# mLSTM: half of the output gate moves to heads 4 to 7, their keys and queries into heads 0 to 3, and a head's sums follow the next scores

## The chip, the cores and the metric

One core of a Trainium2 chip runs the whole program; the other cores are idle. The metric is the device time of one execution in microseconds (us). The engines of the core work side by side, each on its own queue of instructions: TensorE (PE, the matrix products; PEld are its weight loads), VectorE (DVE), ScalarE (ACT), GpSimd (POOL) and SyncE (SP), which issues the loads of the weights.

## The reference, cut to what matters

A trunk of two layers over 512 tokens and 1024 features. Each layer is half a SwiGLU feed-forward, a mixer, and another half feed-forward. The mixer of the first layer is an mLSTM with 8 heads, that of the second a sparse attention (NSA) whose keys and values are computed once, between the two. The mLSTM, in the parts that the change touches:

```python
proj = h @ w_in
q, k, v, ig, fg, og = split(proj)              # 8 heads: q, k of 64, v of 128 columns; og 1024
log_f = log_sigmoid(fg + b_f); b = cumsum(log_f)
D = b[t] - b[s] + log_i[s]                     # for s <= t
W = exp(D - m_t) * (q @ k.T)
num = W @ v + ...                              # and the state carried over chunks
den = sum(W, -1) + ...
h_out = rmsnorm(num / max(abs(den), exp(-m_t)))
return (h_out * sigmoid(og)) @ w_out
```

Between the layers, blocks of the keys and of the values are compressed: `silu(flat @ w1) @ w2`.

## The kernel before

All tokens of the sequence stay in SBUF, transposed: `h[b]` holds 128 features by 512 tokens. Products are made exact to nearly float32 by splitting each operand into a high part and a remainder (`split`: the high part on ScalarE, the difference on VectorE) and adding three matmuls, hi x hi, hi x lo and lo x hi (`mm3`). Weights go the same way: `load_weight` fetches a strip of 512 KB with a DMA on SP into one of two buffers `wraw`, ScalarE writes `whi`, VectorE `wlo`, three buffers each; a strip is asked for two ahead of its use.

The program is written as generators whose steps are one `mm3` or so. `weave(main, fill, ratio)` runs `main` and puts `ratio` steps of `fill` behind each of its steps, so that TensorE has other products while a chain of small work runs on the other engines. The instruction scheduler of the framework may then still change the order within an engine.

In the mLSTM the stages follow each other like this: the input gate products and the first keys and queries; `gates()`, a long chain of row operations on VectorE that ends in `um` (rows of the decay exponents), which TensorE transposes into `pnm`; `project_qk(0)` (keys and queries of heads 0 to 3), `project_v(0)`; then `heads(0)` (heads 0 to 3), filled by `project_og()` (the output gate, eight strips of eight steps); the sigmoids of all eight strips; `project_qk(1)`; `project_v(1)` with `finish(0)`; `heads(1)` (heads 4 to 7), filled by `project_out(0)` (the output projection of heads 0 to 3, 32 steps); `finish(1)`; `project_out(1)`.

A head does this: `S`, the scores, on TensorE; `decay(h + 1)` brings the next head's exponents (`pnm`, then `dg` on VectorE and `E` on ScalarE); VectorE multiplies `E` by `S`; `split` gives `Wh` and `Wl`; GpSimd adds the four strips of `E` into the first (L486); TensorE multiplies by v into `pn`; ScalarE copies that to `num` and squares it to `sqn`. `total` then splits the sums of `E` and `sqn` into `th` and `tl` (ScalarE, VectorE) and adds them with one matmul each into the bank `dm`, so four `dm` matmuls a head. `finish` reads `dm`, makes the scale of each token, and for each head scales `num` (VectorE), multiplies by `sig` (GpSimd, L533) and splits it into `yhi` and `ylo`, which lie in the same eight buffers as the mixer's input x (`xhi`, `xlo`).

`kv()` runs beside the feed-forward `ffn2`: it compresses the blocks in steps between which the feed-forward fills in. `nsa()` begins with `project_q(0)` and the scale `rc` of the tokens from the sum of squares.

## Time and profile before

| | us |
|---|---|
| median of 3 runs | 2067.87 (2067.59 to 2068.0) |
| the profiled execution | 2072.25 |
| its span, first to last instruction | 2070.5 |
| TensorE busy | 2032.7 (98%) |
| VectorE busy | 1155.9 (56%) |
| ScalarE busy | 782.3 (38%) |
| GpSimd busy | 161.1 (8%) |

The profile is of one execution; its times of single instructions and stretches belong to the 2072.25 us, while the runs are timed without it. The mean granted clock of TensorE is 0.996. Matmuls are pipelined: a row's length is longer than the distance to the next one's start, and a busy TensorE can still run below its peak.

### The profile page before, as it was taken

Reading aid. Unit: us, or ns where it says so; the run is one execution under the profiler, and the core shown is the slowest. Engines: PE = TensorE matmul, PEld = TensorE weight load, DVE = VectorE, ACT = ScalarE, POOL = GpSimd, SP = SyncE. Lnnn points to the kernel's source line nnn. Section 1 sums busy time; section 2 is a strip of 40 time slices with the busy share of each in tenths; the row PEclk is TensorE's granted clock in tenths of the full one; section 3 lists DMA queues with packets and bytes.
Section 4 is the critical chain, followed back from the end, with each engine's and each line's share of the span. In section 5 each row is a group of like instructions: output and inputs, shape, how many; then the busy total and the mean of one; then the engine's idle time right before and its main releaser. Section 6 shows DMA issues by size and latency. Waiting matters only on the chain.

```text
span 2070.5 us, 24480 instructions
## 1 busy us (share of the span) xinstructions
PE 2032.7 (98%) x9460; PEld 1666.6 (80%) x9460; DVE 1155.9 (56%) x2044; ACT 782.3 (38%) x1296; POOL 161.1 (8%) x171
## 2 busy tenths in 40 slices
PE   8999999999989999999999999999999999999999
PEld 6888888778768888888887888887778788888887
DVE  6434445765874444445566434446899985444443
ACT  5323223445653222234343322223667663223231
POOL 1000000011220000000101000001333310000000
PEclk9999999999999999999999999999999999999999
DMA  4232323323112323333333332323111112323322
GB/s 160 92 102 91 102 94 91 94 84 100 62 62 92 99 95 97 97 99 97 100 101 125 104 100 86 108 92 100 45 55 42 42 52 93 100 93 97 98 98 94
DMA packets 56468, 188.12 MB, mean 91 GB/s; under 512 B 6816, under 2 KB 7456, under 8 KB 56352
## 3 DMA queue, kind: packets, MB, share of 16 engines
q1 hardware_dynamic: 55392, 184.47, 27.9%
q8 instruction: 74, 1.21, 0.2%
q0 software_dynamic: 384, 1.05, 0.2%
q10 hardware_dynamic: 576, 1.05, 0.1%
q14 instruction: 42, 0.34, 0.1%
HBM read 177.10 MB, written 2.10 MB: 87 GB/s over the span
## 4 chain that ended last, share of the span: by engine, by line
PE 89%; DVE 6%; ACT 2%; issue 1%; POOL 1%; DMA 0%; SPq 0%; ACTq 0%; DVEq 0%; POOLq 0%
PE pmm L142 79%; PE S L142 3%; PE po L142 2%; PE pt L879 1%; PE vps L142 1%; PE paux L142 1%; DVE wlo L124 1%; POOL E L486 1%; DVE qh L762 0%; DVE pr L845 0%; DVE rq L219 0%; DVE ptl L152 0%; PE dm L142 0%; ACT xhi L186 0%; DVE Wl L152 0%
## 5 line engine op out<-in xcount | busy, mean ns | idle before, releaser
L123 ACT ACTIVATE whi<-wraw 128x1024 fp32r<-128x1024 f32 (+4 forms) x399 | 359.9, 916 | 995.4 <-PE pmm L142 821.2
L142 PE MATMUL pmm<-xhi,whi 128*128 128x512 f32 x1672 | 657.6, 393 | 7.7 <-ACT whi L123 7.7
L142 PE MATMUL pmm<-xlo,whi 128*128 128x512 f32 x1672 | 653.9, 391 | 0.0
L142 PE MATMUL pmm<-xhi,wlo 128*128 128x512 f32 x1672 | 653.8, 391 | 0.0
L124 DVE TENSOR_TENSOR wlo<-wraw,whi 128x1024 fp32r<-128x1024 f32 (+4 forms) x399 | 421.0, 1065 | 79.2 <-ACT whi L123 70.7
L142 PEld LDWEIGHTS pmm<-xhi,whi 128*128 128x128 f32 x1672 | 314.5, 188 | 70.6 <-ACT whi L123 8.9
L142 PEld LDWEIGHTS pmm<-xhi,wlo 128*128 128x128 f32 x1672 | 314.3, 188 | 66.8 <-DVE wlo L124 1.1
L142 PEld LDWEIGHTS pmm<-xlo,whi 128*128 128x128 f32 x1672 | 314.6, 188 | 61.8
L142 PE MATMUL pmm<-ghi,wlo 128*128 128x512 f32 x704 | 273.9, 389 | 0.0
L142 PE MATMUL pmm<-ghi,whi 128*128 128x512 f32 x704 | 273.9, 389 | 0.0
L142 PE MATMUL pmm<-glo,whi 128*128 128x512 f32 x704 | 273.9, 389 | 0.0
L270 DVE TENSOR_TENSOR fu<-pmm,r 128x512 f32<-128x512 f32 x88 | 60.8, 691 | 260.5 <-PE pmm L142 260.3
L308 DVE SCALAR_TENSOR_TENSOR h<-pmm,h 128x512 f32<-128x512 f32 x96 | 66.2, 691 | 250.1 <-PE pmm L142 250.1
L268 DVE TENSOR_TENSOR ft<-pmm,r 128x512 f32<-128x512 f32 x88 | 60.8, 690 | 174.2 <-PE pmm L142 174.2
L142 PEld LDWEIGHTS pmm<-glo,whi 128*128 128x128 f32 x704 | 132.2, 188 | 27.5
L142 PEld LDWEIGHTS pmm<-ghi,whi 128*128 128x128 f32 x704 | 132.2, 188 | 27.4
L142 PEld LDWEIGHTS pmm<-ghi,wlo 128*128 128x128 f32 x704 | 132.2, 188 | 27.4
L197 POOL TENSOR_TENSOR ssq<-ssq,sq 128x512 f32<-128x512 f32 x18 | 27.6, 1531 | 1019.5 <-ACT sq L196 1019.5
L151 ACT ACTIVATE ghi<-ft 128x512 fp32r<-128x512 f32 x88 | 55.7, 633 | 72.9 <-DVE ft L271 72.8
L846 ACT ACTIVATE pr<-pr,nx 128x512 f32<-128x512 f32 (+3 forms) x128 | 70.6, 554 | 8.6 <-DVE pr L845 7.9
L152 DVE TENSOR_TENSOR glo<-ft,ghi 128x512 fp32r<-128x512 f32 x88 | 60.4, 686 | 14.7 <-ACT ghi L151 14.7
L845 DVE TENSOR_SCALAR_CACHE_REDUCE pr<-S,cn 128x512 f32<-128x512 f32 (+3 forms) x128 | 66.1, 537 | 2.6 <-PE S L142 2.5
(299 smaller groups left out, 2068.3 us busy)
## 6 DMA issues: line engine op xcount, KB each, us to landing
wraw<-in_ffn_in SPq DMA_DIRECT2D x176, 512.0 KB, 3.5
wraw<-in_ffn_out SPq DMA_DIRECT2D x64, 448.0 KB, 3.3
wraw<-in_ffn_out SPq DMA_DIRECT2D x32, 512.0 KB, 3.6
wraw<-in_m_qk SPq DMA_DIRECT2D x8, 512.0 KB, 3.4
wraw<-in_m_v SPq DMA_DIRECT2D x8, 512.0 KB, 3.6
wraw<-in_m_og SPq DMA_DIRECT2D x8, 512.0 KB, 3.5
wraw<-in_m_out SPq DMA_DIRECT2D x8, 512.0 KB, 3.5
wraw<-in_kv_t SPq DMA_DIRECT2D x8, 512.0 KB, 3.5
```

The lines of the kernel that those rows point to most:

```text
L123: nc.scalar.activation(hi[:p, c], raw[:p, c], AF.Copy)
L124: nc.vector.tensor_tensor(lo[:p, c], raw[:p, c], hi[:p, c].bitcast(F32), op=ALU.subtract)
L142: self.nc.tensor.matmul(out, lhsT, rhs, start=start, stop=stop)
L151: self.nc.scalar.activation(hi, src, AF.Copy)
L152: self.nc.vector.tensor_tensor(lo, src, hi.bitcast(F32), op=ALU.subtract)
L197: (nc.gpsimd if b < 4 else nc.vector).tensor_tensor(t, t, sq, op=ALU.add)
L268: nc.vector.tensor_tensor(t, pa, r, op=ALU.mult)
L270: nc.vector.tensor_tensor(u, pb, r, op=ALU.mult)
L308: nc.vector.scalar_tensor_tensor(h, po[j], 0.5, h, op0=ALU.mult, op1=ALU.add)
L486: nc.gpsimd.tensor_tensor(E[:, sb * P:T], E[:, sb * P:T], E[:, SEG[sb]:SEG[sb] + T - sb * P], op=ALU.add)
L845: TS(s, S[:, i, :n], cc, None, op0=ALU.mult, op1=ALU.min, accum_out=nx[:, i:i + 1])
L846: nc.scalar.activation(s, s, AF.Exp, bias=nx[:, i:i + 1], scale=-1.0, accum_out=z[:, i:i + 1])
```

## The change

The two stops of `gates()` are new: the generator halts before `um`'s transposes, and 20 steps of `project_v(0)` are placed ahead of these. `project_og` takes a half, four strips. The filling work of `heads(0)` is og's strips 0 to 3 and then `project_qk(1)` (64 steps, as before with eight strips of og); that of `heads(1)` is og's strips 4 to 7 and then `project_out(0)`, at 1.05 steps for each step of the heads, in place of 0.4. The sigmoids come in two groups of four, the second behind `heads(1)`, with a table load of its own. `total` no longer issues its matmuls; `add_sums` does, behind the scores of the next head. In `kv()` and `nsa()` the stops between steps change.

```diff
             def gates():
                 ...
                 TS(t2, t2, -1.0, None, op0=ALU.mult)
+                yield
                 nM = pair("nM", t2)
                 up = ps_nm()[:, :160].rearrange("p (t c) -> p t c", t=NTB)
                 ...
-                return nM, uc, e2
+                yield nM, uc, e2
-            def project_og():
-                for m in range(KB):
+            def project_og(half):
+                for m in range(4 * half, 4 * half + 4):
             def heads(half):
                 first = 4 * half
-                E = decay(first)
+                E, sums = decay(first), []
                 def total(row, src, last, *tags):
                     hi, lo = (self.sp.tile([P, T], F32R, name=n, tag=t, bufs=k) for n, (t, k) in zip(("th", "tl"), tags))
                     self.split(src, hi, lo)
-                    for t in (hi, lo):
-                        self.mm(d, hot[:, 39 - row:167 - row], t, row == first and t is hi, last and t is lo)
+                    sums.append((row, hi, lo, last))
+                def add_sums():
+                    while sums:
+                        row, hi, lo, last = sums.pop(0)
+                        for t in (hi, lo):
+                            self.mm(d, hot[:, 39 - row:167 - row], t, row == first and t is hi, last and t is lo)
                 for h in range(first, first + 4):
                     ...
                         yield
+                    add_sums()
                     nE = decay(h + 1) if h < first + 3 else None
                     ...
                     yield
+                add_sums()
+                yield
-            og, out0 = project_og(), project_out(0)
             qk0 = project_qk(0)
             for _ in range(KB):
                 next(qk0)
             r = self.rstd_rows(rc, ps_nm())
-            nM, uc, e2 = gates()
+            g = gates()
+            next(g)
             run(qk0)
-            run(project_v(0))
-            weave(heads(0), og, 1.5)
-            run(og)
-            for m in range(KB):
-                tc.keep_in_program_order(nc.scalar.activation(sig[m], sig[m], AF.Sigmoid))
-            run(project_qk(1))
+            v0 = project_v(0)
+            for _ in range(20):
+                next(v0)
+            nM, uc, e2 = next(g)
+            run(v0)
+            def sigmoids(half):
+                for m in range(4 * half, 4 * half + 4):
+                    tc.keep_in_program_order(nc.scalar.activation(sig[m], sig[m], AF.Sigmoid))
+            rest = chain(project_og(0), project_qk(1))
+            weave(heads(0), rest, 1.45)
+            run(rest)
+            sigmoids(0)
             weave(project_v(1), finish(0), 0.25)
-            weave(heads(1), out0, 0.4)
-            weave(finish(1), out0, 1)
-            run(out0)
+            rest = chain(project_og(1), project_out(0))
+            weave(heads(1), rest, 1.05)
+            sigmoids(1)
+            weave(finish(1), rest, 4)
+            run(rest)
             run(project_out(1))
         # kv: three stops where one was, ahead of the first weight's products (w1)
                     self.split(F.rearrange("p i h c -> p i (h c)"), Fh, Fl)
-                    yield
+                    for _ in range(3):
+                        yield
         # kv: two stops behind the silu, three behind hh
                 nc.scalar.activation(hid[:n], hp[:n], AF.Silu)
-                yield
+                for _ in range(2):
+                    yield
                 ...
                 self.split(ht.rearrange("p k h g c -> p k h (g c)"), hh, hl)
-                yield
+                for _ in range(3):
+                    yield
         # nsa
             rc, var = self.rstd_columns(ssq, ps_t())
+            q1 = project_q(1)
+            for _ in range(4):
+                next(q1)
             run(q0)
             ...
-            for _ in project_q(1):
-                front.steps(0.6)
+            for _ in q1:
+                front.steps(1.2)
```

The order of instructions differs from before within the mLSTM, in the compression beside `ffn2`, and in NSA from its start on. Three places in it:

TensorE at the gates, before: `vps` are the products of v, `um` the rows to be transposed into `pnm`. 52 matmuls of v stand ahead of the transposes.

```order
L142 MATMUL vps<-whi,xlo 128x512
L142 MATMUL vps<-whi,xhi 128x512
L379 MATMUL pnm<-cst,um 128x40 x4
L142 MATMUL vps<-wlo,xhi 128x512
L142 MATMUL vps<-whi,xlo 128x512
```

After, the same place, the transposes between other products of v:

```order
L143 MATMUL vps<-wlo,xhi 128x512
L143 MATMUL vps<-whi,xlo 128x512
L381 MATMUL pnm<-cst,um 128x40 x4
L143 MATMUL vps<-whi,xhi 128x512
L143 MATMUL vps<-wlo,xhi 128x512
```

The transposes stand behind 60 matmuls of v in place of 52.

TensorE among heads 4 to 7, before, from the end of one head's `pn` on (`S` scores, `dm` the sums, `pnm<-nM` the next head's exponents, `pmm` filling work):

```order
L142 MATMUL pn<-Wh,vl 128x256
L142 MATMUL dm<-th,hot 128x512
L142 MATMUL pnm<-nM,sel 128x512
L142 MATMUL pmm<-ylo,whi 128x512
L142 MATMUL dm<-tl,hot 128x512
L142 MATMUL pmm<-yhi,wlo 128x512
L142 MATMUL pmm<-yhi,whi 128x512
L142 MATMUL pmm<-ylo,whi 128x512
L142 MATMUL pmm<-yhi,wlo 128x512
L142 MATMUL S<-qh,kk 128x512
L142 MATMUL S<-ql,kk 128x512
L142 MATMUL dm<-th,hot 128x512
```

The first sum of the head stands right behind its `pn`. After, from the last two matmuls of a head's scores on:

```order
L143 MATMUL S<-qh,kk 128x256
L143 MATMUL S<-ql,kk 128x256
L143 MATMUL pmm<-xhi,whi 128x512
L143 MATMUL pmm<-xlo,whi 128x512
L143 MATMUL pmm<-xhi,wlo 128x512
L143 MATMUL dm<-th,hot 128x512
L143 MATMUL dm<-tl,hot 128x512
L143 MATMUL dm<-th,hot 128x512
L143 MATMUL dm<-tl,hot 128x512
L143 MATMUL pnm<-nM,sel 128x512
L143 MATMUL pmm<-xhi,whi 128x512
```

The four `dm` matmuls of a head were spread from behind its own `pn` into the next scores; now they stand together behind the next head's scores, ahead of `pnm`.

VectorE among heads 4 to 7, before, in one head's stretch (`tl` and `Wl` remainders of a split, `dg` the exponents on the diagonal, `E` times the scores, `h` the residual):

```order
L483 TENSOR_TENSOR E<-E,S 128x512
L450 SCALAR_TENSOR_TENSOR dg<-pnm,uc,cst 128x128
L483 TENSOR_TENSOR E<-E,S 128x512
L152 TENSOR_TENSOR tl<-sqn,th 128x512
L450 SCALAR_TENSOR_TENSOR dg<-pnm,uc,cst 128x128
L483 TENSOR_TENSOR E<-E,S 128x256
L152 TENSOR_TENSOR Wl<-E,Wh 128x512 x2
L450 SCALAR_TENSOR_TENSOR dg<-pnm,uc,cst 128x128
L152 TENSOR_TENSOR Wl<-E,Wh 128x256
```

Nothing of the filling work stands there. After, at the head in which the output projection of heads 0 to 3 begins:

```order
L491 TENSOR_TENSOR E<-E,S 128x512
L441 TENSOR_TENSOR sig<-pmm,r 128x512
L125 TENSOR_TENSOR wlo<-wraw,whi 128x512 x2
L153 TENSOR_TENSOR ylo<-num,yhi 128x512
L491 TENSOR_TENSOR E<-E,S 128x512
L153 TENSOR_TENSOR ylo<-num,yhi 128x512
L491 TENSOR_TENSOR E<-E,S 128x256
L153 TENSOR_TENSOR ylo<-num,yhi 128x512
L452 SCALAR_TENSOR_TENSOR dg<-pnm,uc,cst 128x128
L153 TENSOR_TENSOR tl<-sqn,th 128x512
L153 TENSOR_TENSOR ylo<-num,yhi 128x512
L452 SCALAR_TENSOR_TENSOR dg<-pnm,uc,cst 128x128
```

The four `ylo` of heads 0 to 3 and the `sig` and `wlo` of og's strips stand among the head's own instructions, where before there were fewer of others. On TensorE, 21 dense matmuls stand between the transposes of `hid` and the first `paux<-hh` of the first compression, where nine stood.

## Rows read from the trace of the kernel before

**Rows 1.** The page: the span, and part 1 of it for TensorE, VectorE, ScalarE and GpSimd (busy us, share of the span, instructions).

```profile
span 2070.5 us, 24480 instructions
...
PE 2032.7 (98%) x9460; PEld 1666.6 (80%) x9460; DVE 1155.9 (56%) x2044; ACT 782.3 (38%) x1296; POOL 161.1 (8%) x171
```

**Rows 2.** The chain of waits over the whole execution, one row of it: start, length in us, engine, tile and line, number of instructions.

```profile
21.89 350.28 PE pmm L142 x1552
```

**Rows 3.** Busy time by stretch of the span. Columns: stretch, its length, then busy us (instructions) of TensorE, its weight loads, VectorE, ScalarE and GpSimd, then the granted TensorE clock, the share of DMA and GB/s.

```profile
372.00:430.00 58.00, 55.52 (x241) 43.87 (x240) 44.50 (x75) 23.10 (x42) 0.09 (x1) 0.94 0.33 101
430.00:495.00 65.00, 63.67 (x295) 51.12 (x294) 43.43 (x72) 34.87 (x76) 10.49 (x12) 1.00 0.20 66
495.00:540.00 45.00, 44.68 (x201) 36.12 (x200) 29.69 (x54) 22.37 (x41) 5.95 (x5) 1.00 0.36 107
540.00:585.00 45.00, 40.73 (x188) 32.30 (x187) 37.35 (x75) 30.33 (x68) 11.26 (x12) 0.96 0.13 46
585.00:620.00 35.00, 30.87 (x125) 23.09 (x124) 26.20 (x40) 17.47 (x28) 10.70 (x7) 0.95 0.22 75
...
1055.00:1105.00 50.00, 46.48 (x226) 38.36 (x225) 29.43 (x41) 21.58 (x36) 3.01 (x2) 0.97 0.37 111
...
1442.00:1460.00 18.00, 16.33 (x95) 12.32 (x93) 10.20 (x33) 7.70 (x10) 3.18 (x3) 1.00 0.30 90
```

**Rows 4.** The timeline at the gates, first TensorE, then VectorE: start, length, engine, line, operation, tiles, shapes; in square brackets the idle time before it and what ended that.

```profile
415.64 0.61 PE L379 MATMUL pnm<-cst,um 40*128 40x40 f32 x4 [2.48 <-DVE um L374]
...
414.81 0.68 DVE L374 TENSOR_TENSOR um<-t,t 8x512 f32<-8x512 f32 x1
```

**Rows 5.** Busy time by stretch around the same place, then among heads 4 to 7, columns as in rows 3.

```profile
413.00:425.00 12.00, 9.52 (x31) 7.54 (x31) 6.48 (x10) 3.16 (x7) 0.00 (x0) 0.72 0.40 131
...
563.00:566.00 3.00, 3.00 (x10) 2.38 (x10) 3.00 (x8) 2.70 (x9) 0.85 (x1) 0.57 0.01 5
```

**Rows 6.** VectorE in 540 to 585 us by line: line, operation, tiles, shapes, count | busy us, mean ns | idle time before.

```profile
L152 DVE TENSOR_TENSOR Wl<-E,Wh 128x512 fp32r<-128x512 f32 (+1 forms) x12 | 9.0, 771 | 0.2 <-ACT Wh L151 0.2
L483 DVE TENSOR_TENSOR E<-E,S 128x512 f32<-128x512 f32 (+1 forms) x12 | 6.9, 590 | 0.0
...
L450 DVE SCALAR_TENSOR_TENSOR dg<-pnm,uc,cst 128x128 f32<-128x128 f32 x16 | 5.5, 344 | 1.7 <-ACT E L452 1.7
...
L152 DVE TENSOR_TENSOR tl<-E,th 128x512 fp32r<-128x512 f32 x4 | 2.8, 692 | 2.0 <-ACT th L151 1.7
```

**Rows 7.** VectorE in 430 to 495 us by line, columns as in rows 6.

```profile
L124 DVE TENSOR_TENSOR wlo<-wraw,whi 128x512 fp32r<-128x512 f32 x16 | 11.6, 749 | 0.0
```

**Rows 8.** The waits: of TensorE in 540 to 585, of its weight loads in 540 to 585, and of its weight loads in 430 to 495 us. Columns: what waited for what, us in total, times, longest.

```profile
PE dm L142 <- ACT th L151: 4.0, 4, 1.6
...
PEld dm L142 <- ACT th L151: 5.5, 5, 1.8
...
PEld pn L142 <- DVE Wl L152: 2.2, 4, 1.0
PEld dm L142 <- DVE tl L152: 1.7, 4, 0.5
```

**Rows 9.** The timeline, columns as in rows 4: ScalarE and TensorE among heads 4 to 7, then a pair on VectorE among heads 0 to 3 with GpSimd beside it, then such a pair among heads 4 to 7.

```profile
560.47 0.63 ACT L151 ACTIVATE th<-E 128x512 fp32r<-128x512 f32 x1 [1.78 <-POOL E L486]
...
561.21 0.57 ACT L497 COPY num<-pn 128x512 f32<-128x512 f32 x1
...
562.47 0.63 ACT L151 ACTIVATE th<-sqn 128x512 fp32r<-128x512 f32 x1
...
561.15 0.50 PE L142 MATMUL dm<-th,hot 128*128 128x512 f32 x1 [1.61 <-ACT th L151]
...
438.06 2.41 DVE L152 TENSOR_TENSOR Wl<-E,Wh 128x512 fp32r<-128x512 f32 x2
...
438.02 2.76 POOL L486 TENSOR_TENSOR E<-E 128x384 f32<-128x384 f32 x3 [65.93 <-DVE Wl L152]
...
564.39 1.28 DVE L152 TENSOR_TENSOR Wl<-E,Wh 128x512 fp32r<-128x512 f32 x2
```

**Rows 10.** VectorE in 495 to 516 us by line, columns as in rows 6.

```profile
L152 DVE TENSOR_TENSOR ql<-qks,qh 64x512 fp32r<-64x512 f32 x4 | 2.7, 682 | 0.1
...
L396 DVE SCALAR_TENSOR_TENSOR qks<-pmm,r 128x512 f32<-128x512 f32 x2 | 1.4, 688 | 2.1 <-PE pmm L142 2.1
```

**Rows 11.** The timeline of GpSimd at the end of the mLSTM, columns as in rows 4.

```profile
593.76 1.66 POOL L533 TENSOR_TENSOR num<-num,sig 128x512 f32<-128x512 f32 x1 [1.29 <-DVE num L532]
```

**Rows 12.** The timeline of ScalarE at the sigmoids, columns as in rows 4.

```profile
492.60 1.28 ACT L562 ACT_TABLE_LOAD   x1
493.89 4.28 ACT L562 ACTIVATE sig<-sig 128x512 f32<-128x512 f32 x8
```

**Rows 13.** The compression: the timeline of TensorE (columns as in rows 4), a stretch (columns as in rows 3), and from the page the loads of the weights in question (count, KB each, us to landing).

```profile
1095.87 0.38 PE L676 MATMUL paux<-cst,hid 124*128 124x124 f32 x2
...
1101.00 0.33 PE L142 MATMUL paux<-hh,wlo 128*128 128x128 f32 x1 [2.21 <-DVE wlo L124]
...
1101.00:1107.00 6.00, 6.00 (x22) 5.02 (x23) 4.11 (x9) 2.23 (x4) 0.40 (x1) 0.72 0.55 175
...
wraw<-in_c_w SPq DMA_DIRECT2D x8, 512.0 KB, 3.6
```

**Rows 14.** The waits of TensorE in 1442 to 1452 us, columns as in rows 8.

```profile
PE pt L142 <- DVE rq L220: 1.7, 1, 1.7
```

More of the change, by code (lines that the diff above doesn't have):

```diff
@@ L2 @@
 from contextlib import ExitStack
+from itertools import chain
 import numpy as np
```

## The prediction

> **What bounds the kernel now.** I first read the page: TensorE is busy for 2032.7 of 2070.5 us, VectorE for little over half of that [rows 1]. So TensorE's work is nearly the whole time, and since the change leaves its matmuls what they are, only two things can move the time: stretches in which TensorE waits, and stretches in which it runs at half its clock. The chain of waits gives the unit for everything below: 1552 dense matmuls of 128x512 in 350.28 us, 0.226 us each, one step of filling work (three of them) 0.68 us [rows 2].
>
> Then I read busy time by stretch, to find where TensorE isn't full [rows 3]. The stretches that the change touches: the gates (372 to 430, 2.5 us idle and a granted clock of 0.94), the first four heads (1.3 us idle), the last four (4.3 us, clock 0.96), the end of the mLSTM (4.1 us, 0.95), the compression (3.5 us, 0.97) and the start of NSA (1.7 us).
>
> The gates show how the two hang together. TensorE stops for 2.48 us until `um` is ready [rows 4], and right behind it the granted clock has a mean of 0.72 over 12 us: its two levels are 1.0 and 0.5 (2.4 and 1.2 GHz), so 12 x 0.28 / 0.5 = 6.7 us ran at half speed and 3.4 were lost [rows 5]. So this stop costs 2.5 + 3.4 = 5.9 us, not 2.5.
>
> **Gates.** The generator now stops behind 20 steps of the v projection, but the order says what that is worth: `um`'s transposes stood behind 52 matmuls of v already, and now stand behind 60. Eight matmuls are 1.8 us. VectorE's chain to `um` is in the same order and ends at 415.49, so 2.48 - 1.81 = 0.67 us of the gap stay. Would the clock still fall? After gaps of 2.48 and 2.21 us it did [rows 4, 13]; a gap of 1.61 us among heads 4 to 7 was followed by 0.57 [rows 5, 9], one of 1.7 us at the start of NSA by 1.00 [rows 3, 14]. So such gaps do either, and I take it that one of 0.67 us keeps the clock: 5.9 - 0.7 = **5.2 us won** (bounds 1.8, the gap alone, and 5.9).
>
> **Heads 4 to 7.** Before, 17.6 steps of filling work lie among them (44 steps of the heads x 0.4). The heads' own columns are 17.5 dense matmuls each: 4 x 17.5 x 0.226 = 15.8 us, with the fill 15.8 + 17.6 x 0.68 = 27.8 us of TensorE. VectorE has there `Wl` 9.0, `E` 6.9, `dg` 5.5 and twice `tl` at 2.8 [rows 6], with three adds to `h` of 0.69 and six `wlo` of 0.75 [rows 7] 33.6 us. VectorE is the longer by 5.8 us, and TensorE waits: 4.0 us in front of `dm` [rows 8]. The chain goes over POOL: `th` starts at 560.47 after 1.78 us of waiting for POOL's sums of `E`, `dm` at 561.15 after 1.61 us of idle TensorE [rows 9]. The clock's 0.96 over 45 us is 3.6 us at half speed, 1.8 us lost [rows 3].
> After the change there are 47 steps (45 x 1.05): 15.8 + 47 x 0.68 = 47.8 us of TensorE. VectorE gains four `sig` (2.8), six more `wlo` (4.5), four `ylo` (2.8): 43.7 us. TensorE becomes the longer engine. The sums stand behind the next head's scores, twelve filling matmuls and 2560 columns of scores after `pn` (2.7 + 1.1 = 3.8 us), while `num`, `sqn` and `th` take 1.89 us from 561.21 to 563.10 [rows 9] and a `tl` 0.69 more [rows 6], 2.6 us in all, so the `dm` waits go: 5.5 us by the weight loads' row [rows 8] and 1.8 us of clock, 7.3 us. From that I take off 1.3 us for a new wait: `yhi` and `ylo` of heads 0 to 3 need the buffers of x, which now come free only with the last strip of og; so they now stand in VectorE's and ScalarE's queues between head 6's `E` and `Wl`, four times 0.69 us ahead of `Wl`. **6.0 us won** (bounds 2.0, if VectorE's 43.7 of 47.8 us still delays `Wl`, and 7.3, without the new wait).
>
> **Heads 0 to 3.** The filling work stays 64 steps; four og strips become four of keys and queries. One of og costs VectorE one 0.69 us, one of keys or queries three (0.69 + 2 x 0.68) [rows 10], so 4 x 1.36 = 5.5 us more, 48.9 us against 15.8 + 64 x 0.68 = 59.3 us of TensorE. ScalarE gains eight splits of some 0.63 us, as `th` [rows 9], and has 34.87 of 65 [rows 3]. The `dm` waits (1.7 us as weight loads see them) go, the `Wl` waits (2.2 us) may grow [rows 8]. I take **1 us won** (bounds 4 won, 3 lost). The stage of og and keys behind these heads ran all but full (44.68 of 45) [rows 3], so removing it earns nothing.
>
> **End of the mLSTM.** The chain pick, scale on VectorE, times `sig` on POOL, `yhi`, `ylo` is in the same order, and POOL waits 1.29 us for each product [rows 11]: its 4.1 us of idle time stay. New are a table load and four sigmoids ahead of the copy of `ds`: 1.28 + 4 x 0.535 = 3.4 us [rows 12], under 14 dense matmuls (3.2 us) that stand between the last `dm` and the transposes of `ds`. **0** (bounds 1 won, 1.4 lost). The Trainium skill's ScalarE: Activation LUTs, section What ACT_TABLE_LOAD costs, puts a switch at about 2.66 us, of which 1.38 is a drain. The trace doesn't show that drain here: the sigmoids start 1.29 us after the load [rows 12]. By the page the sum would be some 1.4 us poorer.
>
> **Compression.** `hh` needs a second weight, whose `wlo` comes late: 5.1 us from the transposes at 1095.87 to the matmul at 1101.00, of which nine dense matmuls covered 2.1; 2.21 us idle, then a clock of 0.72 over 6 us: 3.4 us at half speed, 1.7 lost [rows 13]. Now 21 stand there, 4.8 us: about 0.4 us stays, and 1.8 + 1.7 = 3.5 us are won. Against it I set 1.4 us: other weights of this part are asked for earlier than their buffers come free, and each takes 3.6 us to land [rows 13]. **2.1 us won** (bounds 4 won, 1 lost).
>
> **NSA's start.** Four steps of the next query strip are put ahead, yet in the order 17 dense matmuls, not 16, stand between the sum of squares and `rc`; the 1.7 us of wait [rows 14] lose 0.23. **0.2 us won** (bounds 1.7 won, 2 lost by the shifted order behind).
>
> **Sum.** 5.2 + 6.0 + 1.0 + 0 + 2.1 + 0.2 = 14.5 us off the profiled execution's 2072.25, which gives 2057.75. The median of the runs is 2067.87, 0.2% lower; scaled by it, 2067.87 x 2057.75 / 2072.25 = 2053.4.
>
> **The rivals.** *VectorE becomes the bound by its neighbour (slower).* The lone double `Wl` at 438.06 took 2.41 us while POOL summed `E` for 2.76 us; another pair at 564.39 took 1.28 us [rows 9]. So two reads of SBUF on VectorE can run 1.9 times as long beside POOL. In heads 4 to 7 two-operand work from SBUF (`Wl`, `tl`, twelve `wlo`, `ylo`) is 9.0 + 5.6 + 9.0 + 2.8 = 26.4 of 43.7 us; it decides once 0.9 x the part beside POOL exceeds 47.8 - 43.7, at 4.6 us. If all of it were hit, VectorE would need 67 us, 20 more than TensorE; in heads 0 to 3, with 9.0 + 5.6 + 11.6 + 5.5 = 31.7 us of such work, 77 us against 59. Each stage loses some 4 us in my sum already, so both at once add 16 + 16 us to it, and the time is 2085; a third of that, 11 us, would still be faster than before. Against it: POOL is busy for only 10.49 and 11.26 us of the two stretches [rows 3], and `Wl` means 771 ns in the second [rows 6]. The Trainium skill, SBUF — State Buffer, section Who interferes with whom, says that a VectorE instruction with two SBUF inputs contends with a GpSimd one that reads SBUF, and that the second fully blocks; by that rule, the 2.41 us agree. Chance 0.05.
>
> *The change doesn't do what it says (same).* The instruction scheduler had already moved `um` behind 52 matmuls, and NSA's gap moves by one matmul. If 0.67 us behind a busy VectorE still drops the clock, heads 4 to 7 keep waiting for `Wl` and the compression's new waits eat its gain, what is left is 1.8 + 2 = 3.8 us less 0 to 3: 2064 to 2067. Chance 0.12.
>
> *Only part of it.* Gates and compression as above, heads 4 to 7 at their lower bound of 2, heads 0 to 3 slower by 1 or so: 5.2 + 2.1 + 2 - 1 = 8.3 us, 2059.6. 2058 to 2063.7, chance 0.2.
>
> *All stalls gone.* Upper bounds in gates, heads 4 to 7, heads 0 to 3 and compression: 5.9 + 7.3 + 4 + 4 = 21.2 us, 2046.7. 2042 to 2048, chance 0.13.
>
> **Numbers.** The main case, 2048 to 2058, has 0.5. A measurement of this kernel can tell about 0.2%, 4.1 us: below 2063.7 counts as faster, 0.83; within 0.12; slower 0.05. The range of 2043 to 2064 leaves out the cases of no change and slower and the far end of the best, 0.2 in all; the likeliest case's own range is 2048 to 2058.
>
> **What would show it.** Gates: the gap in front of the `um` transposes under 1 us, and no stretch at 0.50 from 410 to 430. Heads 4 to 7: no `dm` row waiting for `th`, clock 1.00. Compression: no 2.21 us wait for `wlo`, 1.00 behind it. End of the mLSTM: the waits for `yhi` as before. I am wrong if VectorE is over 90% busy among heads 4 to 7 while TensorE waits for `Wl`, or if a half-speed stretch follows a gap under 1 us.

## The result and the profile after

| | us |
|---|---|
| median of 5 runs after | 2058.58 (2056.02 to 2059.89) |
| median of 5 runs before, on the same chip | 2068.0 (2067.59 to 2073.43) |
| ratio | 0.9948, interval 0.9933 to 0.9962 |
| the profiled execution after | 2058.29, its span 2056.5 |

The change made the kernel 0.5% faster, 9.4 us of the median; 14.5 had been forecast. Single executions of one kernel differ here by some 4 us with the granted clock: of the 53 executions of the kernel before in the experiments' comparisons, the 10 at a mean clock of 1.000 have a median of 2067.51, the 6 at 0.996 one of 2071.66. The profile on which the forecast rests was one at 0.996.

The page after, beside [rows 1] the span and TensorE's busy time:

```profile
span 2056.5 us, 24485 instructions
...
PE 2027.4 (99%) x9460; PEld 1663.7 (81%) x9460; DVE 1154.1 (56%) x2044; ACT 783.3 (38%) x1297; POOL 161.9 (8%) x171
```

Busy time by stretch after (columns as in rows 3): the gates, heads 0 to 3, the stretch through heads 4 to 7, and the end of the mLSTM.

```profile
413.00:425.00 12.00, 10.38 (x47) 8.36 (x48) 8.66 (x14) 5.18 (x10) 0.00 (x0) 1.00 0.50 165
...
433.00:494.00 61.00, 60.95 (x289) 49.80 (x287) 42.88 (x71) 37.39 (x76) 10.46 (x12) 1.00 0.30 87
494.00:566.00 72.00, 71.92 (x337) 57.77 (x335) 55.53 (x102) 44.43 (x93) 17.07 (x17) 1.00 0.20 66
...
575.00:606.00 31.00, 26.31 (x110) 19.90 (x109) 23.47 (x34) 16.84 (x26) 10.09 (x7) 1.00 0.20 68
```

The gates show 1.00 for [rows 5]'s 0.72. In the stretch through the heads TensorE is idle for 0.05 of 61 and 0.08 of 72 us; before it was 1.3 of 65 and 4.3 of 45 [rows 3]. The end, 26.31 busy of 31.00, waits 4.7 us where it waited 4.1.

The waits after (columns as in rows 8): TensorE at the gates, its weight loads among all heads, TensorE at the end of the mLSTM.

```profile
PE vps L143 <- DVE wlo L125: 1.7, 1, 1.7
...
PEld pn L143 <- DVE Wl L153: 1.8, 8, 0.3
PEld dm L143 <- DVE tl L153: 0.4, 1, 0.4
PEld dm L143 <- ACT th L152: 0.4, 1, 0.4
...
PE pmm L143 <- ACT yhi L152: 2.8, 2, 1.5
```

The gates' wait has another name: `wlo` of the second strip of v's weights, 1.7 us, in place of `um`, 2.48 us [rows 4]. The wait of `dm` for `th`, 5.5 us [rows 8], is 0.4.

TensorE's work as a whole is the same, so the distance between two of its rows shows what a stage takes, once the matmuls between them are counted. From the first `pn` of head 0 to the transposes of the second `ds`, before:

```profile
437.09 0.40 PE L142 MATMUL pn<-Wh,vh 128*128 128x512 f32 x1
...
580.40 0.44 PE L514 MATMUL pnm<-cst,ds 40*128 40x40 f32 x4
```

and after:

```profile
432.59 0.43 PE L143 MATMUL pn<-Wh,vh 128*128 128x512 f32 x1
...
565.60 0.44 PE L524 MATMUL pnm<-cst,ds 40*128 40x40 f32 x4
```

580.40 - 437.09 = 143.31 us became 565.60 - 432.59 = 133.01. The busy time between these rows (columns as in rows 3), before and after:

```profile
437.08:580.39 143.31, 137.40 (x624) 109.90 (x623) 101.36 (x175) 81.49 (x168) 27.70 (x29) 0.99 0.23 74
...
432.58:565.59 133.01, 132.88 (x619) 107.59 (x618) 98.56 (x172) 81.83 (x168) 27.52 (x29) 1.00 0.25 76
```

Five matmuls fewer lie between them after the change, 5 x 0.226 = 1.1 us: eight of the output projection now stand behind the second row, and three of the filling work, which stood ahead of the first, lie between the two. So 1.1 of the 10.3 us is work that has only moved.

### The profile page after: what moved, and what is told of

Its sections match the earlier page's. It is cut to its first block, busy times and chain, and to the rows that moved or that the text cites. A ratio compares the mean times of both kernels' runs of the same rounds, so it can differ in the third digit from the quotient of the medians.

```text
span 2056.5 us, 24485 instructions
## 1 busy us (share of the span) xinstructions
PE 2027.4 (99%) x9460; PEld 1663.7 (81%) x9460; DVE 1154.1 (56%) x2044; ACT 783.3 (38%) x1297; POOL 161.9 (8%) x171
## 3 DMA queue, kind: packets, MB, share of 16 engines
q0 software_dynamic: 384, 1.05, 0.2%
q10 hardware_dynamic: 576, 1.05, 0.1%
## 4 chain that ended last, share of the span: by engine, by line
PE 92%; DVE 4%; ACT 2%; issue 1%; DMA 1%; POOL 0%; SPq 0%; ACTq 0%; POOLq 0%; DVEq 0%
PE pmm L143 82%; PE S L143 3%; PE po L143 2%; PE pt L902 1%; PE paux L143 1%; PE vps L143 1%; PE pn L143 1%; DVE wlo L125 1%; PE dm L143 0%; PE pt L143 0%; ACT whi L124 0%; DVE pr L868 0%; ACT pth L152 0%; PE pg L143 0%; DMA wraw<-in_ffn_in 0%
## 5 line engine op out<-in xcount | busy, mean ns | idle before, releaser
L124 ACT ACTIVATE whi<-wraw 128x1024 fp32r<-128x1024 f32 (+3 forms) x399 | 360.3, 916 | 992.8 <-PE pmm L143 817.5
L125 DVE TENSOR_TENSOR wlo<-wraw,whi 128x1024 fp32r<-128x1024 f32 (+3 forms) x399 | 420.0, 1062 | 76.0 <-ACT whi L124 65.2
```

What stands on the lines that cost most here:

```text
L124: nc.scalar.activation(hi[:p, c], raw[:p, c], AF.Copy)
L125: nc.vector.tensor_tensor(lo[:p, c], raw[:p, c], hi[:p, c].bitcast(F32), op=ALU.subtract)
```

## The experiments

Each ratio is against the kernel before on the same chip. Where two changed kernels of different comparisons are set beside each other, their medians are meant; those of the kernel before were 2068.0 to 2070.0 in these, so a difference of 1 to 2 us between them counts only where the traces show its place. A ten-thousandth of a ratio is 0.2 us.

**The gates alone.** The kernel before with this edit:

```diff
-            nM, uc, e2 = gates()
+            g = gates()
+            next(g)
             run(qk0)
-            run(project_v(0))
+            v0 = project_v(0)
+            for _ in range(20):
+                next(v0)
+            nM, uc, e2 = next(g)
+            run(v0)
```

> The kernel before with the stop in the gates alone. Theory: eight matmuls more ahead of the transposes leave a wait of 1.7 us at the same place, now for wlo of the second v strip, but without a stretch at half clock, and that is what the change got here: 3.5 to 4.2 us less than before, 2064. Rival: the wait has only changed its name and the clock falls as before: 2067 to 2068, and the gain of the change lies in the heads.

Measured: 2067.35 against 2069.1, ratio 0.9995 (0.9986 to 1.0004): no change that can be told. That is the rival's time, but not its reason, since the clock didn't fall. The timeline of TensorE (columns as in rows 4): the gates' wait, the two rows that bound the heads, and the compression's wait.

```profile
414.52 0.50 PE L142 MATMUL vps<-wlo,xhi 128*128 128x512 f32 x1 [1.68 <-DVE wlo L124]
...
433.20 0.39 PE L142 MATMUL pn<-Wh,vh 128*128 128x512 f32 x1
...
576.06 0.44 PE L515 MATMUL pnm<-cst,ds 40*128 40x40 f32 x4
...
1096.77 0.33 PE L142 MATMUL paux<-hh,wlo 128*128 128x128 f32 x1 [2.21 <-DVE wlo L124]
```

And the stretch behind that last wait (columns as in rows 3).

```profile
1097.00:1103.00 6.00, 6.00 (x31) 4.91 (x31) 5.43 (x8) 3.30 (x5) 2.01 (x1) 1.00 0.50 175
```

The compression's 2.21 us wait is exactly as before [rows 13], and behind it the clock is 1.00 where rows 13 have 0.72. The heads, whose code is that of before, take 576.06 - 433.20 = 142.86 us here, and nowhere among them does the clock fall: its mean over the whole execution is 1.000. Before took 143.31 with one, so that stretch cost 0.45 us there, not the 1.8 that the forecast charged. The busy time between the two rows here shows why:

```profile
433.19:576.05 142.86, 135.72 (x624) 108.84 (x623) 101.29 (x175) 81.39 (x168) 27.72 (x29) 1.00 0.24 74
```

With the same 624 matmuls TensorE is idle for 7.1 us here and was for 5.9 before: the half-speed stretch made its matmuls longer and its waits shorter, as long as VectorE set the pace.

**The heads alone.** The changed kernel with gates, compression and NSA as before.

```diff
             g = gates()
             next(g)
+            nM, uc, e2 = next(g)
             run(qk0)
-            v0 = project_v(0)
-            for _ in range(20):
-                next(v0)
-            nM, uc, e2 = next(g)
-            run(v0)
+            run(project_v(0))
```

The edits that take back the compression and NSA's start are shown with their own runs below.

> The kernel before with the change's moves in the heads alone (og halves, keys and queries, sums behind the next scores); gates, compression and NSA as before. Theory: nearly all of the gain lies here, since from the first pn to ds of the second half the changed kernel took 133.0 us where before took 143.3: 8 to 10 us faster than before, 2059 to 2061. Rival: heads and gates need each other, the heads alone give 4 to 6 us, 2063 to 2065.

Measured: 2059.93 against 2070.0, ratio 0.9954 (0.9941 to 0.9966). The timeline of TensorE: the gates' wait and the two rows that bound the heads.

```profile
416.79 0.41 PE L381 MATMUL pnm<-cst,um 40*128 40x40 f32 x4 [2.48 <-DVE um L375]
...
434.50 0.43 PE L143 MATMUL pn<-Wh,vh 128*128 128x512 f32 x1
...
567.53 0.44 PE L524 MATMUL pnm<-cst,ds 40*128 40x40 f32 x4
```

The stretch at the gates:

```profile
413.00:425.00 12.00, 9.52 (x45) 7.60 (x44) 9.19 (x14) 4.48 (x10) 0.00 (x0) 1.00 0.39 132
```

The heads take 567.53 - 434.50 = 133.03 us, 9.8 less than the 142.86; without the 1.1 us of moved work (619 matmuls here too) that is 8.7, nearly the whole result. And the gates' wait of 2.48 us is here to the hundredth as before, yet the clock behind it is 1.00.

**The sums right behind their own head.** The changed kernel with:

```diff
                     sums.append((row, hi, lo, last))
+                    add_sums()
```

> The changed kernel with each head's sums right behind its own products again; the fill of the heads stays as changed. Theory that the fill makes the gain in heads 4 to 7 (47.8 us of TensorE over 43.7 us of VectorE): at most 1.5 us slower than the changed kernel, 2059 to 2060, since other matmuls lie around dm. Rival, that the sums make it: the dm waits for th come back, 3 to 6 us slower, 2062 to 2064.

Measured: 2064.81 against 2069.1, ratio 0.9974 (0.9965 to 0.9983), 6.2 us above the changed kernel: just above the rival's 2062 to 2064. The waits of the weight loads among all heads:

```profile
PEld dm L143 <- ACT th L152: 3.9, 5, 1.7
PEld dm L143 <- DVE tl L153: 3.3, 9, 0.5
```

The timeline's two bounding rows:

```profile
432.58 0.43 PE L143 MATMUL pn<-Wh,vh 128*128 128x512 f32 x1
...
572.03 0.44 PE L525 MATMUL pnm<-cst,ds 40*128 40x40 f32 x4
```

With all the filling work in place, `dm` still waits 7.2 us as the weight loads see it, and the heads take 139.45 us. About 1.7 of these belong to a half-speed stretch in this profile (526 to 532 us, a mean clock of 0.82 and then 0.61 over 3 us each).

**The old filling work.** The changed kernel, with the sums behind the next scores as changed, and:

```diff
-            rest = chain(project_og(0), project_qk(1))
-            weave(heads(0), rest, 1.45)
-            run(rest)
-            sigmoids(0)
+            og, out0 = chain(project_og(0), project_og(1)), project_out(0)
+            weave(heads(0), og, 1.45)
+            run(og)
+            sigmoids(0)
+            sigmoids(1)
+            run(project_qk(1))
             weave(project_v(1), finish(0), 0.25)
-            rest = chain(project_og(1), project_out(0))
-            weave(heads(1), rest, 1.05)
-            sigmoids(1)
-            weave(finish(1), rest, 4)
-            run(rest)
+            weave(heads(1), out0, 0.4)
+            weave(finish(1), out0, 1)
+            run(out0)
```

> The changed kernel with the old filling work: all eight og strips in heads 0 to 3, then eight sigmoids, keys and queries of heads 4 to 7 as a stage of their own, 0.4 steps of the output projection in heads 4 to 7; the sums follow the next scores as changed. Fill theory: VectorE is the longer engine among heads 4 to 7 again, 33.6 over 27.8 us, so 5 to 8 us slower than the changed kernel, 2064 to 2067. Rival, the sums make it: 2058 to 2060.

Measured: 2065.28, ratio 0.9983 (0.9974 to 0.9991), 6.7 us above the changed kernel. The waits of TensorE in 500 to 575 us:

```profile
PE dm L143 <- ACT th L152: 5.0, 5, 1.6
```

The busy time through heads 4 to 7:

```profile
512.00:573.00 61.00, 55.66 (x259) 44.06 (x259) 49.32 (x92) 37.05 (x80) 17.21 (x17) 1.00 0.18 59
```

TensorE is idle for 5.3 of these 61 us, nearly all of it in front of `dm`.

So this theory and its rival are both right in part: with either move alone, the heads keep more than half of their loss (139.45 and, by the same two rows, 140.95 us against 133.01; the first with the 1.7 us of half clock, the second with 627 matmuls between its rows for 619, 1.8 us). Behind the next scores the sums find cover only if there is filling work, and filling work doesn't cover a `dm` that stands right behind its `pn`.

**Less filling work among heads 4 to 7.** The changed kernel with NSA's start as before and:

```diff
-            weave(heads(1), rest, 1.05)
+            weave(heads(1), rest, 0.9)
```

> The changed kernel with NSA's start as before and 0.9 in place of 1.05 filling steps for each step of heads 4 to 7, so that seven more steps (4.6 us) are left for the end of the mLSTM. Theory: TensorE then has 43.2 us among these heads against 43.7 of VectorE; waits come back there (1 to 3 us) and the end gains 1 to 2.5: within 1.5 us of the run with NSA's start alone put back, 2055 to 2057. Rival: the sums behind the next scores are what counts, VectorE's budget isn't, and the end's waits go: 2053 to 2054.5.

Measured: 2058.98 against 2069.46, ratio 0.9947 (0.9934 to 0.9961), 3.1 us above the run with NSA's start alone put back, below, and above both the theory's and the rival's range. The waits of TensorE through heads 4 to 7 and the end:

```profile
PE pmm L143 <- DVE h L559: 2.5, 1, 2.5
PE dm L143 <- ACT th L152: 1.8, 2, 1.4
```

The busy time through heads 4 to 7:

```profile
494.00:565.00 71.00, 68.74 (x316) 53.90 (x317) 52.78 (x98) 43.06 (x91) 16.93 (x17) 1.00 0.19 60
```

Seven steps fewer bring `dm` waits of 1.8 us back, and 71.00 - 68.74 = 2.3 us of idle time for the 0.08 above: these waits came back when TensorE's 47.8 us fell to 43.2 against VectorE's 43.7, as the theory had it. The steps help little at the end, where a `pmm` waits 2.5 us for VectorE to free its bank and, behind that wait, this profile's clock has a mean of 0.72 over 584 to 590 us (1.7 us lost), which is part of the 3.1.

**The compression as before.** The changed kernel with the three edits in `kv` taken back, of which this is the first:

```diff
-                    for _ in range(3):
-                        yield
+                    yield
```

> The changed kernel with the stops of the compression as before. Theory of the forecast's sum: the 2.21 us wait for wlo comes back, the new weight waits go: 2 us slower than the changed kernel, 2060 to 2061. Rival: the 80.5 us from the first kfb to hid became 91.6 for work that only moved, and the wait of 1.56 us there eats the gain: within 1 us of the changed kernel.

Measured: 2061.01 against 2070.0, ratio 0.9961 (0.9948 to 0.9973), 2.4 us above the changed kernel. TensorE's waits from 1010 to 1100 us in this run:

```profile
PE paux L143 <- DVE wlo L125: 2.2, 1, 2.2
PE paux L143 <- ACT whi L124: 1.3, 1, 1.3
```

In the changed kernel:

```profile
PE paux L143 <- ACT whi L124: 2.9, 2, 1.6
```

The change removes 2.2 us of waiting for `wlo` and adds 1.6 us for `whi`. By waits alone that is 0.6 us. By TensorE's rows it is 1.5: from the first row of the feed-forward `ffn2` to the transposes of `rc`, this run takes 1434.65 - 605.40 = 829.25 us and the changed kernel 1433.26 - 605.50 = 827.76, with 3738 matmuls and a clock of 1.00 in both; TensorE is idle for 6.1 and 5.1 us of them. What is left of the 2.4 lies behind these rows, where this profile has a half-speed stretch that the changed kernel's hasn't (a mean clock of 0.72 over 1434 to 1440 us, 1.7 us).

**NSA's start as before.** The changed kernel with:

```diff
-            q1 = project_q(1)
-            for _ in range(4):
-                next(q1)
             run(q0)
 ...
-            for _ in q1:
-                front.steps(1.2)
+            for _ in project_q(1):
+                front.steps(0.6)
```

> The changed kernel with NSA's start as before. Theory: the changed order there costs more than the one matmul it gains: after it, the trace has a 0.99 us wait for cp and a half-speed stretch at 1451 that before had not, together 2 to 3 us; so 1 to 3 us faster than the changed kernel, 2056 to 2057. Rival: half-speed stretches in NSA come and go from execution to execution, whatever the order: equal to the changed kernel within 1 us.

Measured: 2055.91 (2055.34 to 2056.75), ratio 0.9936 (0.9923 to 0.9948), 2.7 us below the changed kernel. The timeline of TensorE in the changed kernel: the transposes of `rc`, a wait, and the first row of the output projection.

```profile
1433.26 1.13 PE L143 MATMUL pt<-cst,rc 128*128 128x128 f32 x8 [1.34 <-DVE rq L221]
...
1449.78 0.63 PE L841 MATMUL pt<-cst,cp 128*64 128x128 f32 x4 [0.99 <-POOL cp L837]
...
1595.70 0.40 PE L143 MATMUL pmm<-olo,whi 128*128 128x512 f32 x1
```

Two stretches of it (columns as in rows 3), one behind that wait, one at the last row:

```profile
1450.00:1456.00 6.00, 6.00 (x29) 4.63 (x27) 5.88 (x26) 4.09 (x13) 4.17 (x4) 0.72 0.54 153
...
1596.00:1602.00 6.00, 6.00 (x33) 5.26 (x31) 5.91 (x24) 3.12 (x12) 3.15 (x5) 0.72 0.11 25
```

The bounding rows with NSA's start as before:

```profile
1433.22 1.13 PE L143 MATMUL pt<-cst,rc 128*128 128x128 f32 x8 [1.67 <-DVE rq L221]
...
1592.79 0.39 PE L143 MATMUL pmm<-olo,whi 128*128 128x512 f32 x1
```

And the whole stretch between them:

```profile
1433.00:1593.00 160.00, 154.13 (x954) 123.79 (x955) 147.05 (x512) 111.56 (x282) 58.67 (x70) 1.00 0.17 45
```

162.44 against 159.57 us, 2.9 more. The wait for `cp` is 0.99 us, in place of two that make 0.4, and 6 x 0.28 = 1.7 us are lost to the clock of 0.72 behind it; the run with NSA's start as before has a clock of 1.00 between these rows. The second stretch at 0.72 lies behind them. All five profiles with the four steps ahead (the changed kernel, the runs of the compression, of the sums, of the old filling work and the next one) have at least one half-speed stretch in NSA; of the eight with NSA's start as before one has. The intervals of the two ratios overlap, so the rows carry more weight here than the medians.

From `rc` to the first row of the last feed-forward (1691.40 in the changed kernel, 1689.00 in this run) all of NSA lies: 258.14 against 255.78 us, 2.4 more. The changed kernel's two stretches cost 1.7 us each if TensorE sets the pace throughout, more than these 2.4. The run of the sums, with one such stretch, takes 256.85. So what NSA loses is in the half-speed stretches, as far as these rows go, and why they come with the changed order is open.

**NSA, one edit at a time.** The changed kernel with the ratio put back to 0.6, the four steps left ahead:

```diff
             for _ in q1:
-                front.steps(1.2)
+                front.steps(0.6)
```

> The changed kernel with 0.6 steps of the fronts for each step of the second query strip, as before, while four steps of that strip stay ahead of the sums. Theory: the ratio of 1.2 is what costs 2.9 us from rc to the output projection in NSA, since it brings the first cp forward (0.99 us wait) and doubles VectorE's work at the start: about 2056, as with both edits undone. Rival: the four steps taken out of the fill leave too little beside the fronts: 2058 to 2059, as changed.

Measured: 2060.61 against 2069.46, ratio 0.9959 (0.9947 to 0.9972): the theory, that all of the loss is the ratio's, is wrong, and the time lies above the rival's range too. The wait for `cp` on TensorE's timeline:

```profile
1453.04 0.63 PE L841 MATMUL pt<-cst,cp 128*64 128x128 f32 x4 [1.26 <-POOL cp L837]
```

And a stretch of ten us at half clock further on, 5 us lost:

```profile
1488.00:1498.00 10.00, 10.00 (x38) 8.63 (x36) 6.12 (x29) 3.60 (x12) 2.48 (x4) 0.50 0.12 46
```

The counterpart, the four steps taken back and the ratio of 1.2 kept, was run on the kernel with the sigmoid's product on VectorE (below, 2054.08):

> As the run with the sigmoid's product on VectorE (2054.1), but of NSA's two edits the ratio of 1.2 stays changed and only the four query steps ahead of the sums are taken back. Theory: the four steps are what costs, since with the ratio put back alone (the steps left ahead) NSA stayed slow: equal to 2054.1 within 1 us, and no wait of 1 us for cp. Rival: either edit costs by itself, since both bring VectorE's fronts forward: 2056 to 2058.

Measured: 2055.07 (2054.6 to 2056.41), ratio 0.9932 (0.9919 to 0.9946), 1.0 us above its base. By the medians most of NSA's 2.7 us comes with the four steps. But the rows of this run's profile say otherwise: from `rc` (1429.55) to the first row of the output projection (1591.77) it takes 162.22 us, as long as the changed kernel, with a wait for `cp` of only 0.35 us, and from `rc` to the last feed-forward 258.40; it has a half-speed stretch too (1478 to 1484 us, 0.72). So which of the two edits brings the loss isn't settled, and that the four steps are missing as cover behind `rc` is not shown.

**The sigmoid's product first, on GpSimd.** NSA's start as before, and in `finish`:

```diff
                 d = dm[half]
+                for h in range(4 * half, 4 * half + 4):
+                    nc.gpsimd.tensor_tensor(num[h], num[h], sig[h], op=ALU.mult)
 ...
-                    nc.gpsimd.tensor_tensor(n, n, sig[h], op=ALU.mult)
```

> The changed kernel with NSA's start as before and, in finish, the product with the sigmoid taken ahead of the scale, so that GpSimd's 1.66 us leave the chain from pick to yhi. Theory: the waits for yhi at the end of the mLSTM (3.2 us beside 37.99 us from ds to the last y) shrink: 1.5 to 3 us faster than with NSA's start alone put back, 2053 to 2054.5. Rival: the chain then waits at ScalarE's or VectorE's queue: 2055 to 2056.

Measured: 2058.05, ratio 0.9946 (0.9933 to 0.9960), 2.1 us slower than without the edit. Neither theory nor rival: the timelines of GpSimd, VectorE and TensorE (columns as in rows 4) show a new wait.

```profile
565.68 5.49 POOL L521 TENSOR_TENSOR num<-num,sig 128x512 f32<-128x512 f32 x4 [7.27 <-ACT sig L577]
...
568.20 3.53 DVE L125 TENSOR_TENSOR wlo<-wraw,whi 128x512 fp32r<-128x512 f32 x2 [1.14 <-ACT whi L124]
...
576.78 0.60 PE L537 MATMUL pnm<-cst,cf 128*8 128x128 f32 x4 [1.29 <-DVE cf L222]
```

The same pair of `wlo` in the changed kernel:

```profile
565.73 1.29 DVE L125 TENSOR_TENSOR wlo<-wraw,whi 128x512 fp32r<-128x512 f32 x2 [1.15 <-ACT whi L124]
```

Beside GpSimd's 5.49 us the pair takes 3.53 us in place of 1.29; `dc` and `cf` behind it are late, and TensorE waits for `cf`.

**Two remainders of the keys on GpSimd as well.** On top of that run:

```diff
-                                self.split(s[a], t[a], t[b])
+                                if half == 0 and j == 1:
+                                    nc.scalar.activation(t[a], s[a], AF.Copy)
+                                    nc.gpsimd.tensor_tensor(t[b], s[a], t[a].bitcast(F32), op=ALU.subtract)
+                                else:
+                                    self.split(s[a], t[a], t[b])
```

> As the run with the sigmoid's product first, and two remainders of the last keys of heads 0 to 3 go from VectorE to GpSimd, so that wlo of the second v strip stands ahead of the last scan. Theory: the 1.7 us wait in the gates is VectorE's queue; it falls to under 0.5 us: 1 to 1.5 us faster than the run with the sigmoid's product first, 2052 to 2053. Rival: the row operations of two SBUF inputs on VectorE are held up by GpSimd for as long: no change.

Measured: 2058.91, ratio 0.9949 (0.9937 to 0.9962), no gain: the rival's case.

The timeline of GpSimd, VectorE (two rows) and TensorE at the gates:

```profile
408.72 7.25 POOL L415 TENSOR_TENSOR kk<-qks,kk 64x512 fp32r<-64x512 f32 x2 [37.19 <-ACT kk L414]
...
410.75 1.77 DVE L373 TENSOR_TENSOR um<-li,t 8x512 f32<-8x512 f32 x1
414.87 1.65 DVE L375 TENSOR_TENSOR um<-t,t 8x512 f32<-8x512 f32 x1
...
416.67 0.42 PE L381 MATMUL pnm<-cst,um 40*128 40x40 f32 x4 [2.29 <-DVE um L375]
```

The two remainders take GpSimd 7.25 us, the row operations for `um` beside them 1.77 and 1.65 us where the last took 0.68 [rows 4], and `um`'s wait of 2.29 us is back. Three `wlo` beside the same work of GpSimd, at 410.17, 412.45 and 414.19, took 0.65 to 0.67 us, so not every VectorE instruction is stretched. That GpSimd is held up as well is argued: its four products above took 5.49 us, these two remainders 7.25, but no run has the remainders alone.

**The sigmoid's product first, on VectorE, for heads 4 to 7 alone.** NSA's start as before, and:

```diff
                 d = dm[half]
+                for h in range(4, 8) if half else ():
+                    TT(num[h], num[h], sig[h], op=ALU.mult)
 ...
-                    nc.gpsimd.tensor_tensor(n, n, sig[h], op=ALU.mult)
+                    if half == 0:
+                        nc.gpsimd.tensor_tensor(n, n, sig[h], op=ALU.mult)
```

> The changed kernel with NSA's start as before and, for heads 4 to 7 alone, the product with the sigmoid taken ahead of the scale on VectorE (four of 0.69 us) in place of GpSimd. Theory: the run with that product on GpSimd lost because its 5.49 us stretched a pair of wlo from 1.29 to 3.53 us; on VectorE nothing is stretched and 1.3 to 1.7 us of GpSimd leave the chain to yhi: 1 to 2.5 us faster than with NSA's start alone put back, 2053.5 to 2055. Rival: the four products stand in VectorE's queue ahead of dc and make cf 2.8 us late, a new wait in front of its transposes: 2056 to 2058.

Measured: 2054.08 (2052.98 to 2054.99) against 2069.46, ratio 0.9925 (0.9913 to 0.9938): the fastest version, faster than both kernels. The four products on VectorE's timeline:

```profile
564.10 2.50 DVE L521 TENSOR_TENSOR num<-num,sig 128x512 f32<-128x512 f32 x4 [1.25 <-ACT sig L579]
```

TensorE's wait for `yhi` from 500 to 606 us:

```profile
PE pmm L143 <- ACT yhi L152: 0.6, 1, 0.6
```

Four products take 2.50 us, and the waits for `yhi`, 2.8 us after the change, are 0.6.

## Why the prediction was right, and where its sizes were off

The direction and the range held; the reason that carries the result, TensorE no longer waiting among the heads, was the forecast's own largest term. Its terms beside what the runs showed:

| term | forecast | measured | from |
|---|---|---|---|
| gates | 5.2 won | 0.7 won | the wait, 2.48 to 1.74 us; the gates alone: no change that can be told |
| heads 0 to 7 | 7.0 won | 8.7 won | 142.86 to 133.03 us, no half clock in either, less 1.1 for five matmuls that moved |
| end of the mLSTM | 0 | about 0.5 won | idle 5.2 us in the gates-alone run, 4.7 after |
| compression | 2.1 won | 1.5 won | the run without it, by rows (2.4 by the medians) |
| NSA's start | 0.2 won | 2.4 lost | the run without it, by rows (2.7 by the medians) |
| sum | 14.5 won | 9.0 won | 9.4 by the medians |

That the sum comes near the medians is partly luck: they carry the clock of each kernel's executions, which the rows of one profile can't give. Of the 14.5 us, 3.4 + 1.8 + 1.7 = 6.9 were clock, taken from one profile at 0.996. And the forecast stayed as near as it did since errors of both signs met: gates 4.5 us and NSA 2.6 too high, heads 1.7 too low.

*Gates.* The step that failed is "I take it that 0.67 us keeps the clock: 5.9 - 0.7". Of the 5.9 us, 3.4 were the price of a half-speed stretch in the one profiled execution. With the same wait of 2.48 us the heads-alone run kept 1.00, so the wait alone doesn't bring that stretch, and taking the wait away can't be credited with it. The bound that was given from below, "1.8, the gap alone", was nearer, and also too high: it left 0.67 us of the wait, and 1.74 stayed. VectorE's queue, full through the whole chain, held `wlo` of the second v strip, and that wait took the place of `um`'s. The forecast asked only what `um` would do, not what else stood in VectorE's queue. Also, the sum was set against an execution at 0.996, 4 us above the median, and scaled by 0.2%, as if those 4 us were spread over the whole; they lie in the half-speed stretches, most of which the change was credited with.

*Heads.* The mechanism is as forecast: VectorE the longer engine before, TensorE after; the sums covered. Both moves are needed, which the forecast put together without saying so. Too low were two sizes. Taking off 1.3 us for the `yhi` and `ylo` among head 6's work was wrong: no such wait is in the changed trace. And 1 us for heads 0 to 3 was too cautious: idle time there is 0.05 us, and the rows of weight loads have `pn` waiting for `Wl` for 1.8 us among all eight heads without a gap on TensorE. The clock's 1.8 us, which were in my 6.0, on the other hand cost only 0.45.

*End of the mLSTM.* As forecast in kind: the chain over GpSimd stays. The 4.1 us of idle time before [rows 3] had a half-speed stretch beside them (0.95), which shortens waits as among the heads; at a clock of 1.00 the gates-alone run is idle there for 5.2 us, so the 4.7 after are no loss. VectorE's version shows that the chain was worth 1.8 us of the median.

*Compression.* Near in sum, 1.5 us by the rows, but not by its terms. Of the 3.5 us credited, 1.7 were clock, and the same wait of 2.21 us kept 1.00 in the gates-alone run. The 1.4 set against them met a new `whi` wait of 1.6 us.

*NSA.* The term that had the wrong sign. The forecast counted the matmuls ahead of `rc` (one more: 0.23 us, and the wait is 1.34 for 1.67 as counted) and gave the order behind it 2 us as a bound only. Behind `rc` lie a longer wait for `cp` and the half-speed stretches, 2.4 us in all, a little beyond that bound.

*The rival of the slower side,* GpSimd's neighbourhood, wasn't decided among the heads, where TensorE is all but full. (Its 2085 us also overstates its own figures: 77 against 59 us less 4 is 14, not 16.) But its mechanism showed twice when an experiment put more work on GpSimd: 3.53 us for 1.29, and 1.77 and 1.65 for 0.68. The Trainium skill's rule (SBUF — State Buffer, section Who interferes with whom) agrees with these rows: each of these VectorE instructions has two inputs in SBUF, as GpSimd's have. The three `wlo` of 0.65 to 0.67 us have two as well, so the rule doesn't say here which instruction is held up.

## What to carry to other kernels

Look for the engine with the longest queue in a stage and count both queues: filling work paid here while TensorE's total stayed above VectorE's, and a result that is waited for must also stand far enough behind its chain; one without the other gave less than half here. A wait that is covered uncovers the next thing in the same full queue, so name that before crediting the gap. Count the matmuls between two rows before taking their distance as a gain. Half-speed stretches of one profiled execution don't come from the waits in front of them alone: price a wait by its gap, and take the clock from several executions. And moving work to a nearly idle GpSimd wasn't free here while VectorE read two operands from SBUF.

## What was not expected of the hardware

The same wait at the same place was followed by half clock in one execution and not in another: 2.48 us at the gates with a mean of 0.72 behind it (before) and 1.00 (heads alone); 2.21 us in the compression with 0.72 (before) and 1.00 (gates alone); 0.99 us for `cp` in NSA with 0.72 (the changed kernel) and 1.00 (the run of the old filling work). In the other direction, the changed kernel's half-speed stretch in 1596 to 1602 us comes while TensorE is busy for 6.00 of 6.00 us, and the last idle time that its timeline shows before it is 0.23 us, at 1586. What sets it off isn't settled by these runs.

Where VectorE sets the pace, half clock on TensorE costs almost nothing: 0.45 us over 143 us of heads, where the clock alone would have cost some 1.8.
